# Attention scores of a two-layer trunk step: from a mix of matmul forms to two stacked 128-row products

## Chip, cores, metric

One core of a Trainium2 chip. The metric is device time in microseconds (us) of one launch, the median over runs of the same kernel.

## What is computed

A two-layer model step over 384 tokens: 128 prompt tokens (context) and 256 latent tokens. Each layer is a half SwiGLU, a mixer, and another half SwiGLU. The mixers hold three attentions of 8 heads with 64 elements each:

```
layer 0: q, k normalised and rotated; context attends to itself, latent to cached context + latent (2 key heads)
layer 1: sliding window with sink (2 key heads), and neighbourhood attention with a bias table (8 key heads)
s = q @ k.T * 0.125 (+ mask or bias);  p = softmax(s);  y = p @ v
```

Layer 0 runs an mLSTM beside its attention. All arithmetic is meant to hold float32 accuracy.

## The kernel before, in words

Tokens stand in three blocks of 128: block T=0 is the context, T=1 and T=2 are the latent tokens. Large products keep accuracy with three products in the rounded format (`float32r`): operand x is split into a rounded part and a remainder, and `mm3` (L371 to L375) sums hi·hi, hi·lo and lo·hi. Each has 128-row weights and 384 or so columns. Weight pieces stream from HBM through `Stream` (L79 on); ScalarE rounds (L116) and VectorE or GpSimd subtract (L117).

The order of the instructions on each engine is made by a scheduler from priorities (program order) and its own estimates. The program's steps in layer 1 are listed in `ORDER1` (L31): `s0 s1 s2 s3 k0 n0 k1 n1 k2 n2 k3 n3 m0`, where s is the sliding-window attention of two heads (`swa`, L1038), k projects the neighbourhood queries (`qk_c`, L1060), n attends with them (`na`, L1043) and m is the first half of the output product (`mix_out`, L709). The scheduler lets later matmuls (`fm`, the projection in `feat_major`; `mo`, the output product) fill gaps of TensorE. Both take their PSUM from the tag `acc`, two banks in turn: fm0, fm1, fm2, fm3, mo0, mo1 and so on. All score and transpose tiles share six banks of the tag `at` (four in layer 0).

An attention step (`attn`, L663) takes two heads j=0, 1 and one token block T: scores into two banks `S`, a mask product (L672, bf16) or a bias add (L676) and sink (L674), then `soft` (L594): maximum on VectorE (L600), exponent on ScalarE (L602), scaling (L606, L608); then transposes on TensorE (L683), copies (L686), the product with the values (L690), and a split of the result (`split_y`). The part from the transposes on is issued one step later. `attn_pair` (L704) runs T=1, T=2 and then T=0.

The scores come in three forms:

- `Stacks` (L615), for layer 0 and the sliding window, T=1 and 2: the query of a head stands as rounded part over remainder in 128 rows (`queries`, L638 and L639), against keys twice, one copy above the other (`kd`, L650 and L651): one product of 128 rows and 384 columns (L660). A second product of 64 rows adds rounded queries times the key remainder `kl` (L661), which holds head group j in rows 64j to 64j+63.
- T=0 of `Stacks` (L657): a plain float32 product of 64 rows and 128 columns, from `q0` (one ScalarE copy, L633).
- Neighbourhood attention (L1052 for T=0; L1054 and L1055 for T=1 and 2): plain float32 products of 64 rows, with 128 columns (context block itself, or cached keys `kcc`) and 256 columns (latent keys). The queries `qc` (L1061) are one ScalarE copy per step, all four kept.

In the profile a plain float32 matmul shows as two records of the same line, a rounded or bf16 one as one record.

Of the kernel before, what the change touches and what calls it, by code (L numbers as in the profile page):

```python
# [12 lines left out]
P = 128  # L13
NT = 384
# [117 lines left out]
def body(ctx, tc, d):  # L132
# [399 lines left out]
    def project(l, dst, scale):  # L532

        ps = [bank(t, f"pk{n}")[:, :NT + 2] for n, t in enumerate(("acc", "acc", "at", "at"))]

        def products(k):
            for n in range(4):
                ip = mm3(ps[n], unit(), H[k], k == 0, k == DC - 1)
            return ip

        R = norm_r(products)
        Rs = rows(R)
        bs = nrm.tile([P, 4, 2], F32, tag="bs", name="bs", bufs=1)
        for n in range(4):
            nc.scalar.activation(bs[:, n], ps[n][:, NT:NT + 2], AF.Copy, scale=scale)
            nc.vector.tensor_tensor(dst[:, n], ps[n][:, :NT], Rs, op=ALU.mult)
# [26 lines left out]
            mm3(p[:, :NT], unit(), [t[:, :NT] for t in h[k]], k == 0, k == DC - 1)  # L573
        return p[:, :NT]

    def work(pool, n, tag="w", size=1040, bufs=4):
        return pool.tile([P, size], F32, tag=tag, name=tag, bufs=bufs)[:, :n]

    def heads(ap, n=64):
# [31 lines left out]
    def split_y(y, hh, hl):  # L611
        nc.scalar.activation(hh, y, AF.Copy)
        nc.vector.tensor_tensor(hl, y, hh.bitcast(F32), op=ALU.subtract)

    class Stacks:  # L615

        def __init__(self, pool, kctx):
            self.q = pool.tile([P, 2048], F32R, tag="qs", name="qs").rearrange("p (i j t) -> p i j t", i=4, j=2)  # L620
            self.q0 = pool.tile([P, 4, P], F32, name="q0s")
            self.k = pool.tile([P, 512], F32, name="ks")
            self.kd = pool.tile([P, 2, NT], F32R, name="kds")
            self.kl = pool.tile([P, NT], F32R, name="kls")
            nc.sync.dma_start(self.k[:, 0:P], kctx)

        def queries(self, src, T):
            p = misc("tr")
            for i in range(4):
                nc.tensor.transpose(p[:, i * P:(i + 1) * P], src[:, i * P:(i + 1) * P], ident)  # L630
            p = p.rearrange("p (i t) -> p i t", i=4)
            if T == 0:
                nc.scalar.activation(self.q0, p, AF.Copy, scale=0.125)  # L633
                return
            t = slice((T - 1) * P, T * P)
            for j in range(2):
                b, o = slice(64 * j, 64 * j + 64), slice(64 - 64 * j, 128 - 64 * j)
                nc.scalar.activation(self.q[b, :, j, t], p[b], AF.Copy, scale=0.125)  # L638
                nc.vector.scalar_tensor_tensor(self.q[o, :, j, t], p[b], 0.125, self.q[b, :, j, t].bitcast(F32),  # L639
                                               op0=ALU.mult, op1=ALU.subtract)  # L640

        def keys(self, src, T):
            p = misc("tr")
            nc.tensor.transpose(p[:, 0:P], src, ident)
            o = 3 * P if T == 0 else T * P
            nc.scalar.activation(self.k[:, o:o + P], p[:, 0:P], AF.Copy)
            if T == 2:
                for j in range(2):
                    b, o = slice(64 * j, 64 * j + 64), slice(64 - 64 * j, 128 - 64 * j)
                    nc.scalar.activation(self.kd[b, j], self.k[b, 0:NT], AF.Copy)  # L650
                    nc.scalar.activation(self.kd[o, j], self.k[b, 0:NT], AF.Copy)  # L651
                    nc.vector.tensor_tensor(self.kl[b], self.k[b, 0:NT], self.kd[b, j].bitcast(F32), op=ALU.subtract)

        def scores(self, S, i, j, T, more):
            b = slice(64 * j, 64 * j + 64)
            if T == 0:
                nc.tensor.matmul(S[:, 0:P], self.q0[b, i], self.k[b, NT:], start=True, stop=True)  # L657
                return
            t = slice((T - 1) * P, T * P)
            nc.tensor.matmul(S[:, 0:NT], self.q[:, i, j, t], self.kd[:, j], start=True, stop=False)  # L660
            nc.tensor.matmul(S[:, 0:NT], self.q[b, i, j, t], self.kl[b], start=False, stop=not more)  # L661

    def attn(pool, i, T, scores, vals, Y, mask=None, sink=None, bias=None):  # L663

        nb = len(vals)
        nk = nb * P
        S = [bank("at", "S") for _ in range(2)]
        for j in range(2):
            scores(S[j], i, j, T, mask is not None)
            if mask is not None:  # L670
                o = P if T == 2 else 2 * P
                nc.tensor.matmul(S[j][:, o:o + P], identb, mask[:, T - 1], start=False, stop=True)  # L672
            if sink is not None:
                nc.vector.tensor_copy(S[j][:, nk:nk + 1], sink(i, j))  # L674
            if bias is not None:
                nc.vector.tensor_tensor(S[j][:, P:nk], S[j][:, P:nk], bias[:, j], op=ALU.add)  # L676
        E = soft(pool, S, nk + (sink is not None), nk)

        def tail():
            pt = [bank("at", "pt") for _ in range(2)]  # L680
            for j in range(2):
# [12 lines left out]
        tails.append(tail)  # L694
        finish(1)
# [7 lines left out]

    def attn_pair(pool, i, scores, vf, vctx, Y, mask=None, sink=None, bias=None):  # L704
        for T in (1, 2):
            attn(pool, i, T, scores, [vctx, lambda j: vf(j, 1), lambda j: vf(j, 2)], Y, mask, sink, bias and bias(T))
        attn(pool, i, 0, scores, [lambda j: vf(j, 0)], Y, None, sink)

    def mix_out(l, Y, last, nxt=None):  # L709
# [18 lines left out]
    def mixer0():  # L728
        with ExitStack() as es:
# [245 lines left out]
                steps[st[0]](int(st[1]))  # L975
            for i in range(4):
                if i == 0:
                    ybh = mp.tile([P, 2048], F32R, tag="qs", name="ybh")[:, :4 * NT].rearrange("p (i t) -> p i t", i=4)
# [21 lines left out]
    def mixer1():  # L1000
        with ExitStack() as es:
            mp = es.enter_context(tc.tile_pool(name="mix1", bufs=1))
            banks(acc="AA", at="BBBBCC")
            kc = mp.tile([P, 4, NT], F32, name="kc")
            h = project(1, kc, 1.0)
            m1v = mp.tile([P, d["m1v"].shape[1]], F32, name="m1v")
            nc.sync.dma_start(m1v, d["m1v"])
            sinkv = m1v[:, 0:8]
            vdc = m1v[:, 8:136]
            kcc = m1v[:, 136:648].rearrange("p (a b) -> p a b", a=4)  # L1010
            vcc = m1v[:, 648:1160]

            sk = Stacks(mp, d["kx1"])
            o = token_major(h, 512)
# [21 lines left out]
            qc = mp.tile([P, 4, NT], F32, name="qc")  # L1036
# [6 lines left out]
            def na(i):  # L1043
                rpb = mp.tile([P, 2, 2, 256], F32, tag="rpb", name="rpb", bufs=2)
                nc.sync.dma_start(rpb, d["rpb"][:, i])
                o = i * P

                def scores(S, i, j, T, more):
                    b = slice(64 * j, 64 * j + 64)
                    q = qc[b, i, T * P:(T + 1) * P]  # L1050
                    if T == 0:
                        nc.tensor.matmul(S[:, 0:P], q, kc[b, i, 0:P], start=True, stop=True)  # L1052
                    else:
                        nc.tensor.matmul(S[:, 0:P], q, kcc[b, i], start=True, stop=True)  # L1054
                        nc.tensor.matmul(S[:, P:NT], q, kc[b, i, P:NT], start=True, stop=True)  # L1055

                attn_pair(mp, i, scores, lambda j, T: vc[:, T, o + 64 * j:o + 64 * j + 64],
                          lambda j: vcc[:, o + 64 * j:o + 64 * j + 64], YC, bias=lambda T: rpb[:, T - 1])

            def qk_c(i):  # L1060
                nc.scalar.activation(qc[:, i], feat_major(h), AF.Copy, scale=0.125)  # L1061

            steps = {"s": swa, "k": qk_c, "n": na, "m": lambda i: mix_out(1, YD, False)}
            for st in ORDER1.split():
# [34 lines left out]
def lay_out(a):  # L1099
# [92 lines left out]
    for hh in range(8):  # L1192
        for dr in range(2):
# [6 lines left out]
    out["m1v"] = np.concatenate([rep(a["sink_l1"]), a["cache_l1_swa_v"][0].reshape(P, P), nk.reshape(P, -1),  # L1200
                                 a["cache_l1_na_v"][0].reshape(P, -1)], 1)

    rpb = a["rpb_l1"]
    bias = np.full((4, 64, 8, 4, 64), -BIG, f)
# [49 lines left out]
```

## Time and profile before

| what | value |
|---|---|
| runs shown | 1565.07 us median of 3 (1564.68 to 1565.58) |
| profiled execution | 1566.02 us, span of its instructions 1564.2 us |
| TensorE (PE) / weight loads (PEld) busy | 1537.1 us (98%) / 1462.5 us (93%) |
| VectorE (DVE) / ScalarE (ACT) / GpSimd (POOL) busy | 1149.8 / 686.0 / 116.1 us |
| attention of layer 0 | about 394 to 494 us of the span |
| attention of layer 1 | about 1147 to 1258 us of the span |

PE and PEld are two rows of the same engine: PEld the loading of a product's weights, PE the product. Matmuls are pipelined, so the records of neighbours overlap, and what a matmul costs is read from the distance of its start to the next one's start, not from its duration. A record starts with its own weight load where that was not done ahead. The granted clock (PEclk) is a share of full speed: 1.00 is 2.4 GHz, 0.50 is 1.2 GHz.

### The profile page before, as it was taken

The numbers are of one execution on the slowest core, as the hardware profiler recorded it, in microseconds if no ns is written. First come the engines' busy times: TensorE is split into PE (matmuls) and PEld (weight loads), VectorE is DVE, ScalarE is ACT, GpSimd is POOL, SyncE is SP. The second block draws the span as 40 slices with busy tenths as digits, with TensorE's granted clock in tenths as the row PEclk, the third lists the DMA queues.
The fourth block names the chain that finished last, engine by engine and source line by source line (L and its number), as shares of the span: only waits on it lengthen the run. The fifth ranks groups of instructions, "written<-read, shape, count | busy, mean of one in ns | idle before, by whom it ended". The sixth has DMA issues, their size and how long they took to land.

```text
span 1564.2 us, 23065 instructions
## 1 busy us (share of the span) xinstructions
PE 1537.1 (98%) x8920; PEld 1462.5 (93%) x8920; DVE 1149.8 (74%) x2291; ACT 686.0 (44%) x1349; POOL 116.1 (7%) x92
## 2 busy tenths in 40 slices
PE   7999999998999999999999999999999999999997
PEld 5999999997778999999999999999977799999997
DVE  3799999976566899999749999974655666555433
ACT  4533343366554543334334343333566654443331
POOL 2100001213011200000100000001110020000010
PEclk9999999999999999999999999999999999999999
DMA  9656566643001566566455655644330223333331
GB/s 371 229 217 212 213 230 231 219 158 110 28 28 68 189 225 228 194 227 218 148 202 202 229 208 210 237 147 158 129 118 29 81 83 133 122 121 135 110 133 41
DMA packets 40126, 256.91 MB, mean 164 GB/s; under 512 B 4432, under 2 KB 8016, under 8 KB 10704
## 3 DMA queue, kind: packets, MB, share of 16 engines
q1 hardware_dynamic: 40016, 255.43, 45.6%
q8 instruction: 70, 1.15, 0.3%
q14 instruction: 40, 0.33, 0.1%
HBM read 252.52 MB, written 2.89 MB: 163 GB/s over the span
## 4 chain that ended last, share of the span: by engine, by line
PE 95%; DVE 2%; issue 1%; ACT 1%; DMA 0%; POOL 0%; POOLq 0%; SPq 0%; DVEq 0%; ACTq 0%
PE gu L373 16%; PE gu L374 16%; PE gu L375 16%; PE fo L373 8%; PE fo L374 8%; PE fo L375 8%; PE pt L690 2%; PE mo L373 2%; PE tm L564 1%; PE tm L565 1%; PE mo L374 1%; PE tm L566 1%; PE mo L375 1%; PE pt L683 1%; PE fm L373 1%; PE fm L374 1%
## 5 line engine op out<-in xcount | busy, mean ns | idle before, releaser
L116 ACT ACTIVATE whi<-raw 128x1024 fp32r<-128x1024 f32 (+2 forms) x378 | 344.5, 927 | 649.6 <-PE gu L374 232.5
L117 DVE TENSOR_TENSOR wlo<-raw,whi 128x1024 fp32r<-128x1024 f32 (+2 forms) x347 | 378.0, 1097 | 145.5 <-ACT whi L116 144.8
L373 PE MATMUL gu<-hh,whi 128*128 128x386 f32 x1408 | 481.7, 342 | 1.4 <-ACT hh L345 1.4
L374 PE MATMUL gu<-hl,whi 128*128 128x386 f32 x1408 | 478.3, 340 | 1.5 <-DVE hl L346 1.5
L375 PE MATMUL gu<-hh,wlo 128*128 128x386 f32 x1408 | 477.0, 339 | 0.0
L251 DVE SCALAR_TENSOR_TENSOR junk<-adaw,cond 128x1024 bf16<-128x1024 f32 x256 | 312.8, 1222 | 1.1 <-DMA adaw<-ada 0.4
L373 PEld LDWEIGHTS gu<-hh,whi 128*128 128x128 f32 x1408 | 266.0, 189 | 4.8 <-issue 2.9
L374 PEld LDWEIGHTS gu<-hl,whi 128*128 128x128 f32 x1408 | 265.7, 189 | 2.1 <-DVE hl L346 2.1
L375 PEld LDWEIGHTS gu<-hh,wlo 128*128 128x128 f32 x1408 | 266.7, 189 | 0.0
L374 PE MATMUL fo<-gl,whi 128*128 128x384 f32 x704 | 235.0, 334 | 0.0
L375 PE MATMUL fo<-gh,wlo 128*128 128x384 f32 x704 | 235.0, 334 | 0.0
L373 PE MATMUL fo<-gh,whi 128*128 128x384 f32 x704 | 234.7, 334 | 0.0
L375 PEld LDWEIGHTS fo<-gh,wlo 128*128 128x128 f32 x704 | 132.1, 188 | 0.0
L374 PEld LDWEIGHTS fo<-gl,whi 128*128 128x128 f32 x704 | 132.1, 188 | 0.0
L373 PEld LDWEIGHTS fo<-gh,whi 128*128 128x128 f32 x704 | 132.1, 188 | 0.0
L287 POOL TENSOR_TENSOR ssq<-ssq,sq 128x384 f32<-128x384 f32 x43 | 50.9, 1184 | 1078.9 <-issue 803.8
L497 DVE COPY bs<-gu 128x2 f32<-128x2 f32 x176 | 27.4, 156 | 79.5 <-PE gu L375 78.8
L501 ACT ACTIVATE s<-s,bs 128x128 f32<-128x128 f32 (+1 forms) x176 | 69.6, 443 | 7.0 <-DVE s L499 6.5
L505 DVE SCALAR_TENSOR_TENSOR gf<-gf,bs,s 128x128 f32<-128x128 f32 (+1 forms) x176 | 65.6, 413 | 2.2
L343 DVE SCALAR_TENSOR_TENSOR hl<-x,sc,hh 128x256 fp32r<-128x256 f32 x96 | 59.7, 647 | 8.3 <-ACT hh L341 8.1
L117 POOL TENSOR_TENSOR wlo<-raw,whi 128x512 fp32r<-128x512 f32 (+2 forms) x31 | 44.9, 1471 | 197.8 <-ACT whi L116 146.0
L341 ACT ACTIVATE hh<-x,sc 128x256 fp32r<-128x256 f32 x96 | 41.9, 445 | 40.2 <-DVE x L379 31.3
(274 smaller groups left out, 1776.6 us busy)
## 6 DMA issues: line engine op xcount, KB each, us to landing
adaw<-ada SPq DMA_DIRECT2D x64, 1024.0 KB, 4.8
raw<-f2i SPq DMA_DIRECT2D x44, 1024.0 KB, 4.7
raw<-f1i SPq DMA_DIRECT2D x43, 1024.0 KB, 4.8
raw<-f1o SPq DMA_DIRECT2D x22, 1024.0 KB, 4.9
raw<-f2o SPq DMA_DIRECT2D x22, 1024.0 KB, 4.7
raw<-mo SPq DMA_DIRECT2D x8, 1024.0 KB, 4.8
aw<-aw SPq DMA_DIRECT2D x7, 1024.0 KB, 7.5
raw<-mic SPq DMA_DIRECT2D x6, 1024.0 KB, 4.9
```

Of the source, the lines that this page charges most:

```text
L116: i1 = nc.scalar.activation(hi[:, a:e], src[:, a:e], AF.Copy)
L117: i2 = (self.nc.gpsimd if j % self.every == 0 else self.sub).tensor_tensor(lo[:, a:e], src[:, a:e], hi[:, a:e].bitcast(F32), op=ALU.subtract)
L251: iv = nc.vector.scalar_tensor_tensor(junk, t, 1.0, ada_state["cond"][:, g], op0=ALU.mult, op1=ALU.mult, accum_out=MOD[l][:, j, g, c:c + 1])
L287: nc.gpsimd.tensor_tensor(ssq_t["t"], ssq_t["t"], sq, op=ALU.add)
L341: ia = nc.scalar.activation(hh[:, a:b], X[c][:, a:b], AF.Copy, scale=SC[l][:, i, g, c:c + 1])
L343: iv = nc.vector.scalar_tensor_tensor(hl[:, a:b], X[c][:, a:b], SC[l][:, i, g, c:c + 1], hh[:, a:b].bitcast(F32), op0=ALU.mult, op1=ALU.su ...
L373: nc.tensor.matmul(out, wh, xh, start=first, stop=False)
L374: nc.tensor.matmul(out, wh, xl, start=False, stop=False)
L375: return nc.tensor.matmul(out, wl, xh, start=False, stop=last)
L501: nc.scalar.activation(s[:, a:e], s[:, a:e], AF.Silu, bias=bs[:, 0, g:g + 1])
L505: iv = nc.vector.scalar_tensor_tensor(gf[:, a:e], gf[:, a:e], bs[:, 1, g:g + 1], s[:, a:e], op0=ALU.add, op1=ALU.mult)
L690: nc.tensor.matmul(y[64 * j:64 * j + 64, :], vals[k](j), PT[:, j, k * P:(k + 1) * P], start=k == 0, stop=k == nb - 1)
```

## The change

Every score becomes two rounded products with 128-row weights, summed in PSUM: the query stack (rounded part over remainder) times the doubled rounded keys, then the same stack times the key remainders over zeros. The remainder tile has one half per j; the other 64 rows are set to zero once, on GpSimd. T=0 uses the same form with 128 columns. Neighbourhood attention gets query stacks `qn` (two buffers) and per-step key stacks (`kdn`, two buffers; remainders `kln`, two tiles); the copy to the other 64 rows is done by GpSimd there and by ScalarE in `Stacks`. The cached keys load into the last 128 columns of `kc` by a DMA of their own, so that the keys of a step are context, latent, latent, cache in one row, and the order of keys and values of that attention is latent, latent, cache. The work tile of layer 1 shrinks from 1040 to 512 columns.

```diff
+    def halves(j):
+        return slice(64 * j, 64 * j + 64), slice(64 - 64 * j, 128 - 64 * j)
+    def stack_q(q, p, j):
+        b, o = halves(j)
+        nc.scalar.activation(q[b], p[b], AF.Copy, scale=0.125)
+        nc.vector.scalar_tensor_tensor(q[o], p[b], 0.125, q[b].bitcast(F32), op0=ALU.mult, op1=ALU.subtract)
+    def stack_k(kd, kl, k, j, dup):
+        b, o = halves(j)
+        nc.scalar.activation(kd[b], k[b], AF.Copy)
+        dup(kd[o], kd[b].bitcast(F32))
+        nc.vector.tensor_tensor(kl[b], k[b], kd[b].bitcast(F32), op=ALU.subtract)
+    def products(S, q, kd, kl, n, more=False):
+        nc.tensor.matmul(S[:, 0:n], q, kd, start=True, stop=False)
+        nc.tensor.matmul(S[:, 0:n], q, kl, start=False, stop=not more)
...
-            self.kd = pool.tile([P, 2, NT], F32R, name="kds")
-            self.kl = pool.tile([P, NT], F32R, name="kls")
+            self.kd = pool.tile([P, 2, 512], F32R, name="kds")
+            self.kl = pool.tile([P, 2, 512], F32R, name="kls")
+            for j in range(2):
+                nc.gpsimd.memset(self.kl[halves(j)[1], j].bitcast(F32), 0.0)
...
-            if T == 0:
-                nc.scalar.activation(self.q0, p, AF.Copy, scale=0.125)
-                return
...
+                stack_q(self.q[:, :, j, T * P:(T + 1) * P], p, j)
...
-                nc.tensor.matmul(S[:, 0:P], self.q0[b, i], self.k[b, NT:], start=True, stop=True)
...
-            nc.tensor.matmul(S[:, 0:NT], self.q[:, i, j, t], self.kd[:, j], start=True, stop=False)
-            nc.tensor.matmul(S[:, 0:NT], self.q[b, i, j, t], self.kl[b], start=False, stop=not more)
+            n, ks = (P, slice(NT, 512)) if T == 0 else (NT, slice(0, NT))
+            products(S, self.q[:, i, j, T * P:(T + 1) * P], self.kd[:, j, ks], self.kl[:, j, ks], n, more)
...
-                nc.vector.tensor_tensor(S[j][:, P:nk], S[j][:, P:nk], bias[:, j], op=ALU.add)
+                nc.vector.tensor_tensor(S[j][:, 0:2 * P], S[j][:, 0:2 * P], bias[:, j], op=ALU.add)
...
+            kc = mp.tile([P, 4, 512], F32, name="kc")
             h = project(1, kc, 1.0)
+            nc.sync.dma_start(kc[:, :, NT:], d["kcc1"])
...
+                kl, kd = kln[i % 2], mp.tile([P, 2, 512], F32R, tag="kdn", name="kdn", bufs=2)
+                for j in range(2):
+                    stack_k(kd[:, j], kl[:, j], kc[:, i], j, lambda d, s: nc.gpsimd.tensor_copy(d, s))
...
-                    if T == 0:
-                        nc.tensor.matmul(S[:, 0:P], q, kc[b, i, 0:P], start=True, stop=True)
-                    else:
-                        nc.tensor.matmul(S[:, 0:P], q, kcc[b, i], start=True, stop=True)
-                        nc.tensor.matmul(S[:, P:NT], q, kc[b, i, P:NT], start=True, stop=True)
+                    n, ks = (P, slice(0, P)) if T == 0 else (NT, slice(P, 512))
+                    products(S, qn[i][:, j, T * P:(T + 1) * P], kd[:, j, ks], kl[:, j, ks], n)
...
             def qk_c(i):
-                nc.scalar.activation(qc[:, i], feat_major(h), AF.Copy, scale=0.125)
+                p = feat_major(h)
+                qn[i] = mp.tile([P, 2, NT], F32R, tag="qn", name="qn", bufs=2)
+                for j in range(2):
+                    stack_q(qn[i][:, j], p, j)
...
-    nc = _bacc.Bacc("TRN2", target_bir_lowering=False, num_devices=1)
+    nc = _bacc.Bacc("TRN2", target_bir_lowering=False, num_devices=1, dynamic_dma_scratch_size=2048)
```

## Rows read from the trace of the kernel before

**Rows 1.** The chain of waits by line, windows 393 to 494 and 1147 to 1258 us.
```profile
by line: PE pv L939 15.1%; PE pt L690 10.6%; PE fm L374 9.3%; PE fm L373 9.1%; PE fm L375 9.0%; PE pt L683 8.2%; PE S L661 5.8%; PE pin L923 5.0%; PE S L660 4.9%; PE D L903 4.0%; PE Sm L931 3.8%; PE Sm L932 3.0%; PE S L657 2.9%; PE D L905 2
...
by line: PE pt L690 15.8%; PE pt L683 11.3%; PE mo L373 7.3%; PE mo L374 6.6%; PE S L1055 6.0%; PE mo L375 5.8%; PE fm L374 5.6%; PE S L1054 5.6%; PE fm L373 5.4%; PE S L661 5.3%; PE fm L375 5.1%; PE S L660 3.9%; PE S L657 2.7%; PE S L672 2
```
**Rows 2.** Windows: length, then busy PE, PEld, DVE, ACT, POOL (instructions), PEclk, DMA.
```profile
378.00:384.00 6.00, 2.06 (x10) 1.09 (x9) 5.91 (x12) 4.63 (x12) 5.09 (x2) 0.98 0.05 14
397.00:404.00 7.00, 7.00 (x32) 5.80 (x31) 2.57 (x9) 3.70 (x14) 0.00 (x0) 0.53 0.00 0
404.00:494.00 90.00, 89.10 (x574) 71.76 (x572) 54.16 (x150) 50.57 (x155) 7.79 (x6) 1.00 0.11 36
...
1185.00:1204.00 19.00, 18.60 (x120) 12.38 (x118) 10.14 (x38) 13.66 (x45) 0.00 (x0) 1.00 0.01 1
1204.00:1258.00 54.00, 52.72 (x375) 40.06 (x373) 35.04 (x103) 35.86 (x114) 2.51 (x2) 1.00 0.17 59
```
**Rows 3.** Timeline of PE, then of PEld, at the first stacked scores of layer 0.
```profile
394.02 0.43 PE L661 MATMUL S<-kls,qs 64*128 64x384 f32 x1
394.38 0.44 PE L660 MATMUL S<-kds,qs 128*128 128x384 f32 x1
...
396.60 2.95 PE L939 MATMUL pv<-va,w 128*128 128x65 f32 x16
...
394.76 0.18 PEld L661 LDWEIGHTS S<-kls,qs 64*128 64x128 f32 x1 [0.19 <-DVE wlo L117]
```
**Rows 4.** Timeline of PE: three-product matmuls in a row, transposes behind them.
```profile
1225.80 0.44 PE L374 MATMUL mo<-ydl,whi 128*128 128x384 f32 x1
1226.08 0.33 PE L375 MATMUL mo<-ydh,wlo 128*128 128x384 f32 x1
...
1227.83 0.34 PE L373 MATMUL mo<-ydh,whi 128*128 128x384 f32 x1
1228.00 0.82 PE L683 MATMUL pt<-kst,E 128*128 128x128 f32 x6
1228.75 0.44 PE L690 MATMUL pt<-PT,vc 128*64 128x128 f32 x4
```
**Rows 5.** Timeline of PE: scores of one head, neighbourhood attention, T=1 or 2.
```profile
1204.88 0.48 PE L1054 MATMUL S<-m1v,qc 64*128 64x128 f32 x2
1205.20 0.59 PE L1055 MATMUL S<-kc,qc 64*128 64x256 f32 x2
1205.73 0.44 PE L683 MATMUL pt<-kst,E 128*128 128x128 f32 x2
```
**Rows 6.** Timeline of PE: scores of one head at T=0, and what follows.
```profile
1155.14 0.48 PE L657 MATMUL S<-ks,q0s 64*128 64x128 f32 x2
1155.56 0.45 PE L373 MATMUL fm<-hh,whi 128*128 128x384 f32 x1
```
**Rows 7.** The chain in order of time: 16 products of the mLSTM at two moments.
```profile
396.67 2.88 PE pv L939 x16
...
409.83 1.73 PE pv L939 x16
```
**Rows 8.** Groups by form, 378 to 394 us; timeline of PE there.
```profile
L639 DVE SCALAR_TENSOR_TENSOR qs<-tr,qs 64x512 fp32r<-64x512 f32 x4 | 2.8, 688 | 2.0 <-ACT qs L638 2.0
L638 ACT ACTIVATE qs<-tr 64x512 fp32r<-64x512 f32 x4 | 2.4, 589 | 0.5 <-DVE qs L639 0.4
...
383.78 1.08 PE L630 MATMUL tr<-kst,w 128*128 128x128 f32 x4 [1.13 <-DVE w L591]
```
**Rows 9.** Layer 1: the query copies; a GpSimd group; windows of tile `mo` (PE, PEld, DVE).
```profile
L1061 ACT ACTIVATE qc<-fm x4: 471/472/475, 1161.7 to 1183.2; 128x384 f32<-128x384 f32 x4
L117 POOL TENSOR_TENSOR wlo<-raw,whi 128x512 fp32r<-128x512 f32 x6 | 7.6, 1286 | 86.1 <-ACT whi L116 47.6 <-PE S L657 26.6 <-issue 11.9
...
1181.00:1212.00 31.00, 4.99 (x21) 3.23 (x21) 0.00 (x0) 1.00 0.09 34
1212.00:1245.00 33.00, 18.01 (x88) 14.81 (x88) 5.84 (x16) 1.00 0.27 97
```

More of the change, by code (lines that the diff above doesn't have):

```diff
@@ L545, in project @@
             nc.scalar.activation(bs[:, n], ps[n][:, NT:NT + 2], AF.Copy, scale=scale)
-            nc.vector.tensor_tensor(dst[:, n], ps[n][:, :NT], Rs, op=ALU.mult)
+            nc.vector.tensor_tensor(dst[:, n, :NT], ps[n][:, :NT], Rs, op=ALU.mult)
             for g, a, b in GR:
@@ L574, in feat_major, with work @@
         return p[:, :NT]
-    def work(pool, n, tag="w", size=1040, bufs=4):
+    wsize = {"w": 1040}
+    def work(pool, n, tag="w", size=None, bufs=4):
+        size = size or wsize[tag]
         return pool.tile([P, size], F32, tag=tag, name=tag, bufs=bufs)[:, :n]
@@ L613, in split_y @@
         nc.vector.tensor_tensor(hl, y, hh.bitcast(F32), op=ALU.subtract)
+    def halves(j):
[12 more added lines that the diff above has]
+        nc.tensor.matmul(S[:, 0:n], q, kl, start=False, stop=not more)
     class Stacks:
         def __init__(self, pool, kctx):
-            self.q = pool.tile([P, 2048], F32R, tag="qs", name="qs").rearrange("p (i j t) -> p i j t", i=4, j=2)
-            self.q0 = pool.tile([P, 4, P], F32, name="q0s")
+            self.q = pool.tile([P, 8 * NT], F32R, tag="qs", name="qs").rearrange("p (i j t) -> p i j t", i=4, j=2)
             self.k = pool.tile([P, 512], F32, name="ks")
-            self.kd = pool.tile([P, 2, NT], F32R, name="kds")
-            self.kl = pool.tile([P, NT], F32R, name="kls")
+            self.kd = pool.tile([P, 2, 512], F32R, name="kds")
+            self.kl = pool.tile([P, 2, 512], F32R, name="kls")
+            for j in range(2):
+                nc.gpsimd.memset(self.kl[halves(j)[1], j].bitcast(F32), 0.0)
             nc.sync.dma_start(self.k[:, 0:P], kctx)
@@ L631, in queries @@
             p = p.rearrange("p (i t) -> p i t", i=4)
-            if T == 0:
-                nc.scalar.activation(self.q0, p, AF.Copy, scale=0.125)
-                return
-            t = slice((T - 1) * P, T * P)
             for j in range(2):
[L637 to L640, printed above, removed]
+                stack_q(self.q[:, :, j, T * P:(T + 1) * P], p, j)
         def keys(self, src, T):
@@ L648, in keys @@
                 for j in range(2):
[L649 to L652, printed above, removed]
+                    stack_k(self.kd[:, j], self.kl[:, j], self.k, j, lambda d, s: nc.scalar.activation(d, s, AF.Copy))
         def scores(self, S, i, j, T, more):
-            b = slice(64 * j, 64 * j + 64)
-            if T == 0:
-                nc.tensor.matmul(S[:, 0:P], self.q0[b, i], self.k[b, NT:], start=True, stop=True)
-                return
-            t = slice((T - 1) * P, T * P)
-            nc.tensor.matmul(S[:, 0:NT], self.q[:, i, j, t], self.kd[:, j], start=True, stop=False)
-            nc.tensor.matmul(S[:, 0:NT], self.q[b, i, j, t], self.kl[b], start=False, stop=not more)
+            n, ks = (P, slice(NT, 512)) if T == 0 else (NT, slice(0, NT))
+            products(S, self.q[:, i, j, T * P:(T + 1) * P], self.kd[:, j, ks], self.kl[:, j, ks], n, more)
     def attn(pool, i, T, scores, vals, Y, mask=None, sink=None, bias=None):
@@ L668, in attn @@
         for j in range(2):
-            scores(S[j], i, j, T, mask is not None)
+            scores(S[j], i, j, T, mask is not None and T > 0)
             if mask is not None:
@@ L705, in attn_pair @@
         for T in (1, 2):
-            attn(pool, i, T, scores, [vctx, lambda j: vf(j, 1), lambda j: vf(j, 2)], Y, mask, sink, bias and bias(T))
+            vals = [lambda j: vf(j, 1), lambda j: vf(j, 2)]
+            attn(pool, i, T, scores, vals + [vctx] if bias else [vctx] + vals, Y, mask, sink, bias and bias(T))
         attn(pool, i, 0, scores, [lambda j: vf(j, 0)], Y, None, sink)
@@ L977, in mixer0 @@
                 if i == 0:
-                    ybh = mp.tile([P, 2048], F32R, tag="qs", name="ybh")[:, :4 * NT].rearrange("p (i t) -> p i t", i=4)
+                    ybh = mp.tile([P, 8 * NT], F32R, tag="qs", name="ybh")[:, :4 * NT].rearrange("p (i t) -> p i t", i=4)
                     ybl = mp.tile([P, 4, NT], F32R, tag="qb", name="ybl")
@@ L1003, in mixer1 @@
             banks(acc="AA", at="BBBBCC")
-            kc = mp.tile([P, 4, NT], F32, name="kc")
+            wsize["w"] = 512
+            kc = mp.tile([P, 4, 512], F32, name="kc")
             h = project(1, kc, 1.0)
+            nc.sync.dma_start(kc[:, :, NT:], d["kcc1"])
             m1v = mp.tile([P, d["m1v"].shape[1]], F32, name="m1v")
@@ L1009, in mixer1 @@
             vdc = m1v[:, 8:136]
-            kcc = m1v[:, 136:648].rearrange("p (a b) -> p a b", a=4)
-            vcc = m1v[:, 648:1160]
+            vcc = m1v[:, 136:648]
+            kln = [mp.tile([P, 2, 512], F32R, name=f"kln{n}") for n in range(2)]
+            for t in kln:
+                for j in range(2):
+                    nc.gpsimd.memset(t[halves(j)[1], j].bitcast(F32), 0.0)
             sk = Stacks(mp, d["kx1"])
@@ L1035, in mixer1 @@
             nc.sync.dma_start(d["vc"], vc[:, 0])
-            qc = mp.tile([P, 4, NT], F32, name="qc")
+            qn = {}
             def swa(i):
@@ L1046, in na @@
                 o = i * P
+                kl, kd = kln[i % 2], mp.tile([P, 2, 512], F32R, tag="kdn", name="kdn", bufs=2)
+                for j in range(2):
+                    stack_k(kd[:, j], kl[:, j], kc[:, i], j, lambda d, s: nc.gpsimd.tensor_copy(d, s))
                 def scores(S, i, j, T, more):
-                    b = slice(64 * j, 64 * j + 64)
-                    q = qc[b, i, T * P:(T + 1) * P]
-                    if T == 0:
-                        nc.tensor.matmul(S[:, 0:P], q, kc[b, i, 0:P], start=True, stop=True)
-                    else:
-                        nc.tensor.matmul(S[:, 0:P], q, kcc[b, i], start=True, stop=True)
-                        nc.tensor.matmul(S[:, P:NT], q, kc[b, i, P:NT], start=True, stop=True)
+                    n, ks = (P, slice(0, P)) if T == 0 else (NT, slice(P, 512))
+                    products(S, qn[i][:, j, T * P:(T + 1) * P], kd[:, j, ks], kl[:, j, ks], n)
                 attn_pair(mp, i, scores, lambda j, T: vc[:, T, o + 64 * j:o + 64 * j + 64],
@@ L1060, in qk_c @@
             def qk_c(i):
-                nc.scalar.activation(qc[:, i], feat_major(h), AF.Copy, scale=0.125)
+                p = feat_major(h)
+                qn[i] = mp.tile([P, 2, NT], F32R, tag="qn", name="qn", bufs=2)
+                for j in range(2):
+                    stack_q(qn[i][:, j], p, j)
             steps = {"s": swa, "k": qk_c, "n": na, "m": lambda i: mix_out(1, YD, False)}
@@ L1199, in lay_out @@
     nk = a["cache_l1_na_k"][0].reshape(P, 4, P).transpose(2, 1, 0)
-    out["m1v"] = np.concatenate([rep(a["sink_l1"]), a["cache_l1_swa_v"][0].reshape(P, P), nk.reshape(P, -1),
-                                 a["cache_l1_na_v"][0].reshape(P, -1)], 1)
+    out["kcc1"] = nk
+    out["m1v"] = np.concatenate([rep(a["sink_l1"]), a["cache_l1_swa_v"][0].reshape(P, P), a["cache_l1_na_v"][0].reshape(P, -1)], 1)
     rpb = a["rpb_l1"]
```

## The prediction

> **What bounds the kernel now.** I read the page's busy shares first (PE 98%, DVE 74%, ACT 44%), then the two attention stretches, since the change touches nothing else. The chain of waits cut to them [rows 1] runs almost wholly over TensorE lines. The reader is to add up the score lines: L661, L660 and L657 are 13.6% of 101 us in layer 0, 13.7 us; L1055, L1054, L661, L660 and L657 are 23.5% of 111 us in layer 1, 26.1 us. The windows [rows 2] then say what stands behind TensorE: in layer 0 DVE is busy 54.2 and ACT 50.6 of 90 us, so there is room; in layer 1, from 1185 to 1258 us, ACT is busy 49.5 and DVE 45.2 of 73 us, so there is less. In one stretch, 378 to 384, TensorE is busy 2.06 of 6 us and DVE 5.91: there DVE is the bound.
>
> Then I read spacings, since a PE record's duration hides the pipelining. Products of one form in a row, 128-row weights and 384 columns, start 0.175 us apart (ten steps from 1226.08 to 1227.83) [rows 4]. The stacked scores, which alternate between 128-row and 64-row weights, start 0.369 us apart (seven steps from 394.02 to 396.60) [rows 3], although they stream the same 384 columns. The weight-load row in the same group tells why: each load begins only after 0.19 us of idling, when the product before is through. The change of height, not the arithmetic, is half of the price. After plain 64-row products, too, the next full product takes 0.28 us to its successor instead of 0.175 (1225.80 to 1226.08) [rows 4].
>
> **The change part by part.**
>
> *Stacked scores, T=1 and 2.* A head costs 2 x 0.369 = 0.74 us now. Two products of equal height cost 0.35 inside a row of such, and 2 x 0.28 = 0.56 where another form stands on either side. The saving lies between 0.18 and 0.39 per head. In layer 0 (4 steps x 2 blocks x 2 heads = 16 heads) both neighbourhoods occur, and I take the middle, 0.29: 4.6 us. In the sliding window each head has the bf16 mask product behind it, so I take the low end: 16 x 0.18 = 2.9 us.
>
> *Neighbourhood attention, T=1 and 2.* A head costs 0.85 us now, four records from 1204.88 to 1205.73 [rows 5]. It becomes the same two products; with a stranger on each side 0.56. 16 x 0.29 = 4.6 us; inside a row of such 16 x 0.5 = 8.0.
>
> *T=0.* 24 heads of 0.42 us now (1155.14 to 1155.56) [rows 6]. They become two rounded products of 128 columns. No row shows one so narrow. The nearest row is that of the transposes: equal weights, 128 columns, 0.125 us apart (six from 1228.00 to 1228.75) [rows 4]; two of them make 0.25, with 0.1 more at each end for the strangers (0.28 less 0.175) 0.45. I take no change. From below 0.25 (a gain of 24 x 0.17 = 4.1), from above two halves of the plain product with both ends, 0.42 + 0.2 = 0.62 (a loss of 4.8).
>
> *The clock.* From 397 to 404 the granted clock is 0.53 [rows 2], so mostly at 1.2 GHz; the same 16 products take 2.88 us there and 1.73 later [rows 7]. What TensorE did just before is the half-idle alternation of [rows 3]. At most 7 x 0.47 = 3.3 us come back if the denser scores keep the clock at 2.4 GHz; nothing, or a loss of half of that, if it falls elsewhere. I take half: 1.6 us back.
>
> *Query stacks at T=0, layer 0.* One ScalarE copy becomes two copies of 64 rows (0.59 each) and two VectorE remainders (0.69 each) [rows 8]. They fall into 378 to 384, where DVE is full and TensorE waits 1.13 us for DVE's rotated queries [rows 8]. No cover there: 2 x 0.69 = 1.4 us lost; nothing if they are placed behind the rotation of T=2. GpSimd's two settings to zero, at most 1.29 us each as the subtraction of twice the rows [rows 9], are hidden if they come before the norm's power steps on GpSimd, and cost up to 2.6 if not. I take 1.4 for all of it.
>
> *Preparation in layer 1.* ScalarE: 4 steps x (2 x 0.59 - 0.47) = 2.8 for queries, 8 x 0.59 = 4.7 for keys [rows 8, 9]. VectorE: 16 remainders of at most 0.69, 11 us. GpSimd: 8 copies and 6 settings to zero of at most 1.29, 18 us on an engine that is nearly idle, ahead of need except in the first steps. Some of ACT's and DVE's part falls before 1185. After it, roughly 5 of ACT's and 7 of DVE's would lie in 73 - 6 = 67 us, which puts both near 80%; in-order engines with chains between them don't overlap fully at that.
>
> *What is queued behind the query stacks.* The plain queries were kept for all four steps, and all four projections were copied by 1183 [rows 9]. Now there are two buffers: the stack of step 2 waits until n0 has read the first, step 3 until n1 has read the second. Until then fm2 and fm3 hold the two banks of `acc`, and `mo` waits for those banks. Of its products 21 ran before 1212 as filler [rows 9], 21 x 0.175 = 3.7 us; they move behind. With the fuller ACT and DVE I take 3.0 us given back in layer 1, between nothing and all of its 2.9 + 4.6 = 7.5.
>
> *At nothing:* the cached keys as a DMA of their own are used 100 us after their issue; the GpSimd scratch size touches no DMA that this program issues; the bias add keeps its size.
>
> **Sum:** -4.6 - 2.9 - 4.6 + 0 - 1.6 + 1.4 + 3.0 = -9.3 us. The profiled execution took 1566.02 us (its span 1564.2), 0.95 above the median of 1565.07. On the median: **1555.8 us**.
>
> **The skill against it.** The spacings show that equal full heights follow each other at 0.175 and unequal ones at 0.369 [rows 3, 4]. The Trainium skill, "TensorE: Matmul & The Clock Gate", section "The mechanism", says that a weight load overlaps with running products only when the two use different row groups. By that rule full-height products would never hide their loads, and the time would be that of the rival with exposed loads below. The trace disagrees [rows 4], so I give it little.
>
> **The rivals.**
>
> *Narrow rounded products are dear.* For: no row shows them below 256 columns. Against: the transposes. At the upper bound +4.8: 1560.6 us.
>
> *Layer 1 keeps nothing.* ACT, DVE and the held banks eat all 7.5: 4.5 more than taken, 1560.3 us. For: ACT at 13.7 of 19 us before n0 [rows 2]. Against: in layer 0 there is room, and it keeps its 4.6.
>
> *Weight loads of scores stay exposed.* The change does not do what it says: the second product of full height still waits. Stacked heads save nothing, neighbourhood heads 16 x (0.85 - 0.74) = 1.8, preparation costs 1.4: 1564.7 us, no difference.
>
> *Slower: the output product loses its cover.* Its place is the `acc` banks. 88 products of `mo` stand between 1212 and 1245 [rows 9]. If they cannot start until n1 is through and n2 and n3 are bound by ACT, they run alone at the end. The point from which it decides: 12.1 + 1.6 - 1.4 = 12.3 us of gain are 70 products. All 88 cost 15.4, and a clock that falls in the gaps some 2 more: 1565.1 - 12.3 + 17.4 = 1570.2 us.
>
> **How the numbers follow.** Forecast 0.58, narrow products 0.14, layer 1 keeps nothing 0.16, exposed loads 0.04, slower 0.08. The forecast's own bounds are 1551 to 1560: toward 1551 if the clock holds and the held banks cost nothing (-3.0 - 1.7), toward 1560 if the clock gives nothing back and the preparation costs its 2.6. To hold 8 in 10 the range takes in the two milder rivals at their upper ends and a little of the heads inside rows: 1549 to 1562.5. A measurement of this kernel can tell about 0.2%, 3.1 us. Faster by more: the forecast, and nearly all of the two mild rivals, 0.84. Within: exposed loads and what is left of those two, 0.08. Slower: 0.08.
>
> **What would show it.** Right: the two new product lines both in the form 128*128, their starts about 0.175 apart inside a head; PEclk 1.00 from 397 to 404; the chain's score lines near 9 us in layer 0; a T=0 head at most 0.45; ACT over 75% between 1185 and the end of n3. Wrong: 0.37 between products of one head (loads exposed); 0.2 or more per product of 128 columns; TensorE idle for microseconds between n0 and n1, with `mo` in a block after n3; or TensorE waiting longer than 3 us for DVE before the first stacked scores.

## The result, and the profile after

| | before | after |
|---|---|---|
| median of the runs | 1565.0 us | 1555.69 us (1554.16 to 1555.86) |
| ratio, 95% interval | 1 | 0.9936 (0.9921 to 0.9952) |
| profiled execution / its span | 1566.02 / 1564.2 us | 1554.16 / 1552.4 us |
| layer 0, first `tm` product to last `mo` product | 205.5 us | 196.6 us |
| layer 1, the same | 168.1 us | 165.8 us |
| all the rest | 1190.6 us | 1190.0 us |

The forecast was 1555.8 us and the time is 1555.7, faster by 9.3 us. The sum came out and its split did not. The layer lengths are read from the starts of the first and the last such product (326.1 and 531.6 us before, 325.1 and 521.7 after in layer 0). Layer 0 gained 8.9 us where 4.8 were forecast, layer 1 2.3 where 4.5 were. The profiled executions lie further apart than the medians (11.9 against 9.3 us), so a single layer's figure may be off by two or three us. One of the four runs of e4 below took 2133.6 us at a much lower granted clock (0.655); its row goes by the other three.

The chain of waits by line of the kernel after, windows 393 to 484 and 1170 to 1246 us, answers to [rows 1]. L636 is the product with the keys, L637 the one with the remainders, L693 and L700 are the transposes and the product with the values.

```profile
by line: PE pv L950 15.8%; PE fm L373 9.7%; PE fm L374 9.4%; PE pt L700 9.4%; PE fm L375 9.4%; PE pt L693 7.1%; PE Sm L942 5.1%; PE S L636 5.0%; PE pin L934 4.9%; PE S L637 4.3%; PE Sm L943 4.0%; PE D L914 3.5%; PE D L916 2.2%; PE pin L936 
...
by line: PE pt L700 16.3%; ACT E L605 10.0%; PE pt L693 7.9%; PE mo L373 7.4%; PE mo L374 6.8%; PE mo L375 6.5%; PE S L636 6.2%; DVE nm L603 5.1%; ACT E L609 4.8%; ACT PT L696 4.6%; issue 4.1%; PE S L637 3.5%; ACT whi L116 2.7%; DVE S L686 
```

In layer 0 the score lines fell from 13.7 us to 9.3% of 91, 8.5 us, and the chain is still TensorE's. In layer 1 it is not: exponents (L605), maxima (L603), scalings (L609) and copies (L696) of the other engines now stand in it with a quarter of the time. Before, none of them was among the lines of that row; nor is one when the window of the kernel before starts at 1170 us, as this one does.

Now the spacing that the change was about: the timeline of PE in layer 0, and one PEld row from the same place.

```profile
395.16 0.34 PE L637 MATMUL S<-kls,qs 128*128 128x384 f32 x1
395.33 0.33 PE L636 MATMUL S<-kds,qs 128*128 128x384 f32 x1
395.50 0.33 PE L637 MATMUL S<-kls,qs 128*128 128x384 f32 x1
395.68 0.33 PE L636 MATMUL S<-kds,qs 128*128 128x384 f32 x1
...
395.51 0.19 PEld L636 LDWEIGHTS S<-kds,qs 128*128 128x128 f32 x1
```

The starts are 0.17 us apart where they were 0.37 [rows 3], and the row of the load names no idle time before it: it begins at 395.51, while another product runs, for a product that starts at 395.68. Two heads at T=0, 128 columns each:

```profile
1208.50 0.22 PE L636 MATMUL S<-kdn,qn 128*128 128x128 f32 x1
1208.56 0.27 PE L637 MATMUL S<-kln,qn 128*128 128x128 f32 x1
1208.67 0.27 PE L636 MATMUL S<-kdn,qn 128*128 128x128 f32 x1
1208.78 0.28 PE L637 MATMUL S<-kln,qn 128*128 128x128 f32 x1
1208.90 0.84 PE L693 MATMUL pt<-kst,E 128*128 128x128 f32 x6
```

Four products, two heads, take 0.40 us, 0.06 to 0.12 each; one plain head took 0.42 [rows 6]. Narrow rounded products are not dear, they are cheaper.

The windows (length, then busy PE, PEld, DVE, ACT, POOL, PEclk, DMA) answer to [rows 2]:

```profile
383.00:390.00 7.00, 6.76 (x25) 5.74 (x26) 3.56 (x7) 4.57 (x13) 0.00 (x0) 0.58 0.45 152
...
397.00:404.00 7.00, 7.00 (x45) 6.41 (x44) 3.37 (x12) 5.08 (x18) 0.00 (x0) 1.00 0.01 2
...
1187.00:1200.00 13.00, 10.06 (x71) 7.23 (x70) 9.96 (x28) 12.09 (x38) 2.06 (x2) 0.92 0.13 42
```

The clock of 397 to 404 is 1.00 now, 2.4 GHz; it was 0.53. And there is a new hole: from 1187 to 1200 TensorE is busy 10.06 of 13 us. Before, it was busy 18.60 of 19 us in the stretch that ended at 1204. TensorE's idle time in layer 1, added over its records, rose from 2.6 to 9.8 us. The tile `mo` in layer 1, first and last start, tells what is missing there:

```profile
L373 PE MATMUL mo<-ydh,whi x32: 331/338/425, 1201.4 to 1229.6; 128*128 128x384 f32 x32
```

No product of the output fills a gap before 1201.4; in the kernel before 21 of them had run by 1212 [rows 9].

### The profile page after: what moved, and what is told of

It reads as the page before. It is cut to its first block, busy times and chain, and to the rows that moved or that the text cites. A ratio compares the mean times of both kernels' runs of the same rounds, so it can differ in the third digit from the quotient of the medians.

```text
span 1552.4 us, 23061 instructions
## 1 busy us (share of the span) xinstructions
PE 1517.2 (98%) x8888; PEld 1458.7 (94%) x8888; DVE 1161.2 (75%) x2311; ACT 694.1 (45%) x1363; POOL 128.4 (8%) x108
## 4 chain that ended last, share of the span: by engine, by line
PE 93%; DVE 3%; ACT 2%; issue 1%; DMA 0%; POOL 0%; POOLq 0%; SPq 0%; DVEq 0%; ACTq 0%
PE gu L373 16%; PE gu L374 16%; PE gu L375 16%; PE fo L373 8%; PE fo L374 8%; PE fo L375 8%; PE tm L564 2%; PE tm L565 2%; PE tm L566 2%; PE pt L700 2%; PE mo L373 1%; PE mo L374 1%; PE mo L375 1%; PE fm L373 1%; PE fm L374 1%
```

## The experiments

Each ratio is to the kernel before, run on the same chip in the same series; "after" is 0.9936. Medians of different series are from different chips, so kernels are compared by their ratios. Layer lengths and sums over one layer are from one profile of each kernel.

| run | median us | ratio (95%) |
|---|---|---|
| e1, four query buffers | 1551.76 | 0.9906 (0.9891 to 0.9921) |
| e3, remainder product on 64 rows | 1577.06 | 1.0067 (1.0052 to 1.0082) |
| e4, zeros alone in the kernel before | 1555.51 | 0.9929 (0.9912 to 0.9945) |
| e5, neighbourhood scores plain | 1552.24 | 0.9910 (0.9893 to 0.9926) |
| e6, two query buffers in the kernel before | 1569.92 | 1.0022 (1.0012 to 1.0032) |
| e7, e1 with T=0 queries last | 1551.63 | 0.9909 (0.9894 to 0.9924) |
| e8, e1 with GpSimd rounding keys | 1551.59 | 0.9907 (0.9893 to 0.9922) |
| e9, e5 with one product for two | 1551.61 | 0.9909 (0.9894 to 0.9924) |
| e10, e1 with half of the key stacks (steps 2 and 3 use those of 0 and 1) | 1551.69 | 0.9910 (0.9896 to 0.9925) |
| e11, e1 with key remainders on GpSimd | 1552.39 | 0.9917 (0.9900 to 0.9933) |
| e12, e1 without the scaling of the neighbourhood exponents | 1549.09 | 0.9895 (0.9879 to 0.9912) |

### Is it the height of the weights? e3 and e4

```diff
 e3, on the kernel after (b: the 64 rows of head group j)
-        nc.tensor.matmul(S[:, 0:n], q, kl, start=False, stop=not more)
+        nc.tensor.matmul(S[:, 0:n], q[b], kl[b], start=False, stop=not more)
...
 e4, on the kernel before
-            self.kl = pool.tile([P, NT], F32R, name="kls")
+            self.kl = pool.tile([P, 2, NT], F32R, name="kls")
+            for j in range(2):
+                nc.gpsimd.memset(self.kl[64 - 64 * j:128 - 64 * j, j].bitcast(F32), 0.0)
...
-            nc.tensor.matmul(S[:, 0:NT], self.q[b, i, j, t], self.kl[b], start=False, stop=not more)
+            nc.tensor.matmul(S[:, 0:NT], self.q[:, i, j, t], self.kl[:, j], start=False, stop=not more)
```

> The changed kernel with the remainder product again on 64 rows only (no zero rows read), everything else kept. Theory (a change of height exposes load and drain): the products of a head are 0.37 us apart again; heads of layer 0 lose 4.8 us, of the sliding window 4, of the neighbourhood attention about 3, and the clock falls again at the first scores of layer 0 (up to 3.3): 1563 to 1569 us. Rival (zeros do not matter, the gain is from the form of the other scores): 1555 to 1557 us.

> The kernel before with one part of the change alone: the key remainders of the stacked scores stand over zeros and the second product has 128 rows; T=0 and the neighbourhood attention stay plain. Theory: layer 0 gains 4.8 us in the scores and up to 3.3 from the clock, the sliding window about 4, and no preparation is added: 1554 to 1557 us, as fast as the whole change. Rival (each part gives its share, as the prediction had it): 4.6 + 2.9 + 1.6 = 9.1 less, minus nothing, is 1556, but then the neighbourhood part must show its own gain when it is taken out of the whole change.

e4, the zeros alone, is as fast as the whole change (0.9929 against 0.9936). The last four of the first eight stacked scores of layer 0 in e4, timeline of PE, with the mLSTM products behind them:

```profile
396.57 0.34 PE L662 MATMUL S<-kds,qs 128*128 128x384 f32 x1
396.75 0.33 PE L663 MATMUL S<-kls,qs 128*128 128x384 f32 x1
396.93 0.33 PE L662 MATMUL S<-kds,qs 128*128 128x384 f32 x1
397.10 0.34 PE L663 MATMUL S<-kls,qs 128*128 128x384 f32 x1
397.27 1.89 PE L941 MATMUL pv<-va,w 128*128 128x65 f32 x16
```

Eight scores in a row and the 16 products behind them stand as in the kernel before; of these only the height differs. The step is 0.175 us instead of 0.369 [rows 3], and the 16 products run at full clock. In layer 0 e4 takes 198.9 us against 205.5, in layer 1 164.4 against 168.1.

e3 went further than its expected range: 1577 us, 11 slower than the kernel before. Its windows:

```profile
1190.00:1205.00 15.00, 13.46 (x77) 9.55 (x77) 7.07 (x29) 11.10 (x36) 0.00 (x0) 0.77 0.01 2
1205.00:1222.00 17.00, 15.04 (x74) 11.32 (x74) 10.45 (x27) 11.32 (x33) 2.07 (x2) 0.70 0.10 31
397.00:404.00 7.00, 7.00 (x44) 5.95 (x45) 3.99 (x13) 5.63 (x18) 0.00 (x0) 1.00 0.01 2
```

Layer 0 takes 204.9 us, so nearly all of its gain is gone. The distances from each score's start to the next start add up to 15.6 us there, against 8.7 in the kernel after: the heights alone account for 6.9 of the 8.3 us. The other part of the expectation did not come: the clock of 397 to 404 stays at 1.00. Layer 1 takes 180.1 us, 12 more than before: there the exposed loads (its score distances are 35.7 us against 24.9), the held banks (below) and a granted clock of 0.70 to 0.77 come together, which the expectation had not put into its sum. What each of them costs was not tried apart.

The Trainium skill ("TensorE: Matmul & The Clock Gate", "The mechanism") lets loads overlap only across different row groups; e4 shows loads of one and the same full height hidden at 0.175 us, so the measurement decides against that rule here. The same section also lets a load run ahead when it goes to the background weight buffer; the runs agree with that, though none of them shows the buffer itself.

### Why layer 1 kept so little: e1, e5, e6

```diff
 e1, on the kernel after
-                qn[i] = mp.tile([P, 2, NT], F32R, tag="qn", name="qn", bufs=2)
+                qn[i] = mp.tile([P, 2, NT], F32R, tag="qn", name="qn", bufs=4)
 e5, on the kernel after: no kdn, kln; queries again one copy
...
+                        nc.tensor.matmul(S[:, 0:2 * P], q, kc[b, i, P:NT], start=True, stop=True)
+                        nc.tensor.matmul(S[:, 2 * P:NT], q, kc[b, i, NT:], start=True, stop=True)
...
 e6, on the kernel before
...
-                nc.scalar.activation(qc[:, i], feat_major(h), AF.Copy, scale=0.125)
+                p = feat_major(h)
+                qn[i] = mp.tile([P, NT], F32, tag="qn", name="qn", bufs=2)
+                nc.scalar.activation(qn[i], p, AF.Copy, scale=0.125)
```

> Four buffers for the query stacks of the neighbourhood attention instead of two, nothing else. Theory (held banks): fm2 and fm3 hold the two acc banks until n0 and n1 have read their queries, so mo cannot fill gaps before 1201 us. With four buffers mo starts near 1181 us, TensorE's idle time in layer 1 (9.8 us in the changed kernel, 2.6 before) falls by half, and the time is 1551 to 1553 us. Rival (full ACT and DVE): the gaps come from ScalarE, which is busy 12.1 of 13 us there; mo may start earlier, but the time stays at 1555 to 1556 us.

> The changed kernel with the neighbourhood attention's scores plain again (one ScalarE copy per step, all four kept, no key stacks); the stacked heads and T=0 of the stacks keep the change. Theory: its 3 us of scores come back, but the banks are free early and ScalarE and VectorE have less to do, so the time is 1553 to 1557 us: the neighbourhood part brings nothing. Rival (the neighbourhood part pays 4.6 us as predicted): 1559 to 1561 us.

> The kernel before, with one line of the change's side effects alone: the plain neighbourhood queries of a step get two buffers instead of all four being kept. No score changes its form. Theory (held banks): fm2 and fm3 hold both acc banks until n0 and n1 have read, mo starts near 1205 instead of 1182 us, TensorE idles about 4 us more in layer 1, and the kernel is 3 to 5 us slower than before (ratio 1.002 to 1.003). Rival (the loss in layer 1 comes from the added work on ScalarE and VectorE): no difference, ratio 0.999 to 1.001.

All three came out for the held banks, though not in every number. The tile `mo` in layer 1, first in e1, then in e6:

```profile
L373 PE MATMUL mo<-ydh,whi x32: 333/338/447, 1170.9 to 1218.3; 128*128 128x384 f32 x32
```
```profile
L373 PE MATMUL mo<-ydh,whi x32: 333/336/446, 1212.2 to 1240.2; 128*128 128x384 f32 x32
```

With four buffers the output product starts at 1170.9 instead of 1201.4; with two buffers alone, put into a kernel whose scores are all as before, it starts at 1212.2, and the kernel is 0.22% slower. That edit costs about 3.5 us by itself (1.9 to 5.0). TensorE's idle time in layer 1 rises by less than expected there, from 2.6 to 4.5 us and not by 4, and the layer from 168.1 to 171.0 us. In e1 the hole is closed, as the same window shows, and its clock is 1.00:

```profile
1187.00:1200.00 13.00, 12.58 (x93) 9.57 (x93) 9.74 (x34) 11.27 (x37) 0.10 (x1) 1.00 0.04 7
```

Idle time fell from 9.8 to 6.1 us, not by a half but by 3.7. e5 says the rest: with plain neighbourhood scores and no stacks for them, the time is that of e1 (0.9910, 0.9906) and below its own expected range. The new form of these scores is worth nothing here; with two buffers it cost about 4 us (0.9936, an interval that just touches that of e1 and overlaps that of e5; e7 to e11, which share their cure, lie at 0.9907 to 0.9917).

Layer 1 step by step: 168.1 us before, 164.4 with the zeros (e4), 162.1 with T=0 in the new form too and the rest of the change but the neighbourhood stacks (e5), 162.6 with these stacks and four buffers (e1), 165.8 with two (the kernel after).

### What limits layer 1 then: e8, e10, e11, e9, e12

From e5 to e1 the distances of the score starts add up to 6.0 us less (25.7 to 19.7), and layer 1 is no shorter (162.1 and 162.6 us). First suspect was the added work. The edits, by what they do to the neighbourhood keys (e8 and e11 pass the engine as an argument):

```diff
 e8:  -        nc.scalar.activation(kd[b], k[b], AF.Copy)
      +        nc.gpsimd.tensor_copy(kd[b], k[b])
 e11: -        nc.vector.tensor_tensor(kl[b], k[b], kd[b].bitcast(F32), op=ALU.subtract)
      +        nc.gpsimd.tensor_tensor(kl[b], k[b], kd[b].bitcast(F32), op=ALU.subtract)
 e10: +                if i < 2:                             (then kdn[i % 2], kln[i % 2])
```

> The kernel with four query buffers, and GpSimd instead of ScalarE rounds the neighbourhood keys (8 copies of 64x512, 0.63 us each on ScalarE). Theory (with the banks free, ScalarE is what still makes TensorE idle 6.1 us in layer 1): 1 to 3 us faster than four buffers alone. Rival (the gaps are the latency of one step's chain, whichever engine): within 0.5 us, or slower since GpSimd's copies take about 1 us each in series.

> Four query buffers, and key stacks of the neighbourhood attention are prepared for steps 0 and 1 alone; steps 2 and 3 use those again (their own keys are left out of the result). That takes away half of the key preparation: 4 copies on ScalarE, 4 on GpSimd, 4 remainders on VectorE. Theory (load): what eats the cheaper scores of this attention is the added work on the other engines, so the time falls by 1.5 to 3 us against four buffers alone (1551.8). Rival (chain): each step's own chain from scores over the exponents to the values sets the pace once TensorE has slack, and the time stays within 0.7 us.

> Four query buffers, and GpSimd computes the remainders of the neighbourhood keys (8 of 64x512, up to 0.81 us each on VectorE). Theory (VectorE's added load is the part that counts): 1 to 2 us faster than four buffers alone. Rival (chain, or GpSimd now late): within 0.7 us, or slower.

None moved the time. ScalarE's busy time in layer 1 fell from 115.6 to 110.7 us in e8, VectorE's from 117.9 to 114.3 in e10, and the layer stayed within 0.7 us. The theory of load falls, for four buffers, as far as intervals of some 2.5 us to either side and these layer lengths can tell. e11 is no test of it: eight remainders of 7.3 us in all left VectorE, but its busy time fell by 1.3 us alone (117.9 to 116.6). The 32 `wlo` took 25.1 us instead of 22.3 and eight `hl` (L365) 7.9 instead of 4.7, and the long ones lie under GpSimd's instructions: an `hl` of 1.55 us has 1.51 us of them beside it, one with none beside it takes 0.34 to 0.48 in e1. Whether ScalarE's work adds to the hole of the kernel with two buffers was not tried apart.

e9 made two plain products of a head into one:

```diff
-                        nc.tensor.matmul(S[:, 0:2 * P], q, kc[b, i, P:NT], start=True, stop=True)
-                        nc.tensor.matmul(S[:, 2 * P:NT], q, kc[b, i, NT:], start=True, stop=True)
+                        nc.tensor.matmul(S[:, 0:NT], q, kc[b, i, P:], start=True, stop=True)
```

> The changed kernel with plain neighbourhood scores, and the two plain products of a head at T=1 and 2 (128 and 256 columns) made one of 384 columns, which the key order latent, latent, cache allows. By the rows a head costs 0.85 us; one plain product of 384 columns saves two weight loads of which one was exposed: 0.75. 16 x 0.1 = 1.6 us less than with two: 1550 to 1551.5 us, faster than both kernels. If loads are hidden anyway, no difference.

A miss. Timeline of PE in e9, one head:

```profile
1215.60 0.91 PE L1066 MATMUL S<-kc,qc 64*128 64x384 f32 x2
1216.44 0.44 PE L693 MATMUL pt<-kst,E 128*128 128x128 f32 x2
```

The head costs 0.84 us, as two products did [rows 5]. PEld in the kernel before, at the two products of [rows 5], tells why:

```profile
1205.09 0.30 PEld L1055 LDWEIGHTS S<-kc,qc 64*128 64x128 f32 x2
1205.72 0.20 PEld L683 LDWEIGHTS pt<-kst,E 128*128 128x128 f32 x2 [0.33 <-ACT PT L686]
```

The second load of the head begins at 1205.09, 0.11 us before its product and with no idle time named before it, so there was little left to save. What is exposed is the load of the other height behind the head, which begins 0.01 us before its product after 0.33 us of idling, and that stays: in e9 it begins with its product, after 0.55 us.

e12 shortened the chain of a step (`scale` is false in the neighbourhood attention):

```diff
-        for j in range(2):
+        for j in range(2 if scale else 0):
...
```

> Four query buffers, and in the neighbourhood attention the scaling of the exponents by the reciprocal sum is left out (so its part of the result is not normalised): 12 ScalarE and 12 VectorE instructions, about 6.5 and 4.5 us, which stand inside the chain from exponents to transposes. Moving 5 us of ScalarE's key rounding off that engine, outside this chain, had changed nothing. Theory (the chain of a step sets the pace where TensorE has slack): 2 to 4 us faster than four buffers alone, 1548 to 1550. Rival (TensorE's own work is still the bound in layer 1): within 0.7 us of 1551.7.

Layer 1 went from 162.6 to 159.6 us and the median to 1549.1, which is in the expected range; by the ratio it is 1.7 us (0.9895 against 0.9906), and the intervals overlap. It speaks for the chain of each step (scores, maximum, exponents, scaling, transposes) and is no proof: the edit also takes 6 us off ScalarE, though taking 5 off in another place had done nothing. The chain of waits by line of e1, 1170 to 1245 us, fits it:

```profile
by line: PE pt L700 20.3%; PE pt L693 9.8%; PE S L636 8.8%; ACT E L605 6.3%; PE mo L373 6.0%; ACT PT L696 5.1%; PE mo L374 5.0%; ACT E L609 4.7%; PE S L637 4.7%; PE mo L375 4.7%; DVE nm L603 4.4%; issue 2.9%; DVE S L686 2.7%; DVE E L611 2.5
```

Links of a step on ScalarE and VectorE still make up a quarter of it. In e5, where the neighbourhood scores are plain, the same chain (1170 to 1243 us) is nearly all TensorE's:

```profile
by line: PE pt L700 20.8%; PE pt L693 14.1%; PE S L1066 13.1%; PE mo L373 11.2%; PE mo L374 9.3%; PE mo L375 8.4%; PE S L1067 4.8%; ACT E L605 3.4%; PE S L636 2.9%; ACT PT L696 2.5%; PE S L1064 2.3%; PE S L637 1.8%; ACT E L609 1.4%; issue 0
```

The 6 us that TensorE saves on scores from e5 to e1 come back as waiting: its idle time in layer 1 goes from 2.9 to 6.1 us, and the distances behind transposes and value products (`pt`) from 33.9 to 38.7.

### Layer 0's query stacks: e7

```diff
...
+                    elif T == 0:
+                        r0 = r
...
+            sk.queries(r0, 0)
...
```

> The kernel with four query buffers, and in layer 0 the query stack of T=0 is issued behind those of T=1 and T=2. Theory (the two remainders of T=0 stand on the bound engine ahead of the rotation of T=2): the first scores come about 1.4 us earlier and the time falls by 1 to 1.5 us against four buffers alone. Rival (the start of the scores there is set by the clock and by ScalarE, not by these two): within 0.5 us.

No difference: layer 0 takes 197.9 us against 197.7. The rival has the time; its reason is not shown. The first stacked score does come earlier, 68.1 us behind the first product of the layer against 69.9, but TensorE had other products to run in its place, so the layer is no shorter.

## Why the prediction came out, step by step

- **Stacked scores, layer 0: right.** 4.6 us forecast; the distances from start to start, added over the 32 records, went from 11.5 to 6.7 us.
- **Stacked scores, sliding window: mechanism right, size low.** 2.9 forecast, 11.2 to 7.1 us. The low end was taken since a mask product follows each head, and 0.28 us was reckoned for both products. They cost 0.26 and 0.19 us: only the one behind a mask product is dearer, the one in front of it is not.
- **Neighbourhood scores: right on TensorE, wrong in worth.** 4.6 forecast; 12.6 to 9.4 us in the kernel after, a half-speed stretch included, and to 8.1 in e1. e5 shows that the time does not follow.
- **T=0: nothing was taken, and something came.** In layer 0 these products went from 2.8 to 2.0 us, in layer 1 from 5.9 to 3.3 in e1 (7.1 in the kernel after, with waits among them). From e4 to e5, which adds this form and the rest of the change but the neighbourhood stacks, the ratio goes from 0.9929 to 0.9910, with intervals that overlap. A head costs 0.25 us in layer 0 now, where the sum had 0.45: the 0.1 us added at each end was wrong. The rival with dear narrow products is out.
- **The clock: half was forecast, more came, and its cause is open.** The fall at 397 is gone. All of layer 0 outside the scores went from 191.2 to 187.9 us, 3.3 less, the whole upper bound; the largest parts are `pv` 15.7 to 14.6, `pt` 18.5 to 17.4 and `pin` 7.7 to 6.7. Not all of it need be the clock. The prediction saw the half-idle alternation ahead of the fall; e3 alternates at the same place and keeps 1.00. The clock still falls before the first scores, from 382.0 to 388.8; TensorE waits at its start alone and is busy 6.76 of the 7 us from 383 on.
- **Query stacks at T=0, 1.4 us lost: about the right size, the named cause not borne out.** From 376 to 388 us TensorE's idle time adds up to 3.9 us before, 3.3 in e4 (T=0 plain) and 4.7 in the kernel after (4.7 to 5.4 in the others with the same layer 0). With VectorE's two remainders out of the way (e7) it is still 4.5, and the layer is no shorter.
- **Given back in layer 1, 3.0 us: the right place, too small.** Of 7.5 forecast for its scores (6.5 measured, T=0 and mask included) 2.3 remained, so 4.2 were given back. e6 puts about 3.5 us on the buffers alone, by the mechanism that the prediction described: fm2 and fm3 hold the banks of `acc`, and `mo` waits. The prediction named ScalarE and VectorE beside it; e8 and e10 take that away for four buffers. ScalarE is busy 42.5 of the 59 us from 1187 to 1246, 72%, where over 75% was the sign of being right; and one sign of being wrong came, TensorE idle for 2.9 us between 1187 and 1200.
- **The slower rival** had this mechanism and the wrong point: the products of `mo` that lost their early place found room beside the steps, 36 of their records from 1201 to 1212 us and 78 from 1212 to 1245, where the chains left TensorE gaps.

So the sum held because layer 0 gained about 4 us more and layer 1 about 2 less than forecast, with the distance between profiled executions and medians on top. An agreement of 0.1 us says nothing about the terms.

## What to carry to other kernels

Products of the same height in a row hid each other's weight loads here (0.175 us apart); with every second one of half the height each load waited for the product before it (0.369 us apart). So filling up with zeros to the full height was worth more than the rows it adds. Where a tile that is filled from PSUM loses buffers, look at who shares that PSUM tag next: the banks stay held until the tile is free, and the loss appears in another product that fills gaps. Take parts of a change out one by one: here the zeros alone gave as much as the whole change, and one number (four buffers, 1551.8 us) beats the change as made. And ask what binds once the cheaper part is cheap: saved TensorE time turned into waiting for the chain of each step.

## What was not expected of the hardware

In the kernel before the granted clock fell from 2.4 to 1.2 GHz at 397 us, just behind eight scores of alternating height; TensorE's row is busy throughout the 4 us ahead of it. In e6, which leaves these scores as they are, it fell at 398; in e4, with equal heights, it did not. That does not make alternation the cause. In e3 the heights alternate at the same place, with two other products in between, and the clock of 397 to 404 is 1.00. And in e4 the clock had come back only at 391.6 us, against 387.2 in the kernel before, so what lies ahead differs too: in both, layer 0 has 10.2 us at half speed in all. Which of these sets the fall was not settled.

The first fall in layer 0 has another length from execution to execution. Nine kernels have the same code in layer 0 (after, e1, e5, e8 to e12 and, but for the order of one step, e7): it lasts 6.8 us in six of them and 10.2 in three. The window of e1:

```profile
381.00:391.00 10.00, 7.14 (x24) 5.75 (x25) 6.57 (x13) 6.81 (x18) 2.10 (x1) 0.50 0.29 107
```

Layer 0 takes 197.6 to 197.7 us in the three and 196.6 to 197.9 in the six: 3.4 us more at half speed cost half a microsecond or so, since TensorE was waiting for other engines for part of it.

Some of VectorE's subtractions took about three times as long under GpSimd's instructions (e11, above: 1.55 us against 0.34 to 0.48), so work moved to GpSimd was in part paid for on VectorE.
